# Moving the last six weight sums of layer 0 from the residual loads into the gates

## The chip, the cores and the metric

The kernel runs on one core of one Trainium2 chip. The metric is the device time of one execution in microseconds (us), as the median of several runs. A core has a matrix engine (PE, with PEld for its weight loads), a vector engine (DVE), a scalar engine (ACT), GpSimd (POOL) and a sync engine (SP). Each engine works its own queue of instructions in order. DMAs are issued from the queues of SP, ACT and POOL and are carried by 16 DMA engines that all of them share.

## What is computed

The reference is a trunk of two residual layers over 528 rows (16 meta tokens and 512 of the sequence) of width 2048. Layer 0 is a convolution branch and a sparse attention branch, each multiplied by a SiLU gate, put side by side and sent through one output projection. Layer 1 is a gated linear recurrence, which this change does not touch.

```python
def even_mixer(hn, w_in, conv_w, ...):
    glu_v, glu_g, gate_a, q, c, gate_b, qi, ki, wi = split_last(hn @ w_in, EVEN_SPLITS)
    ...
    a_out = jax.nn.silu(layer_norm(u, ln_g, ln_b)) * jax.nn.silu(gate_a)
    ...
    b_out = b_out * jax.nn.silu(gate_b)
    return jnp.concatenate([a_out, b_out], axis=-1) @ w_out

for layer in range(DEPTH):
    hn = rms_norm(h, norm_gain[layer])
    ...
    h = h + y
```

## The kernel before

All matrices are held transposed: 128 channels on the partitions, up to 528 rows along the free dimension. To keep fp32 precision, each operand is split into two fp16 halves (hi and lo), and a product is three matmuls (lines 270 to 272 in a "stripe", line 1069 in a "product" of 24 matmuls). A weight slab of 128 output channels comes from HBM into a `w32` buffer, is scaled and rounded by ACT (line 207, `wh`), and the rest is taken by DVE (line 209, `wl`).

**The output projection of layer 0** handles the 16 slabs of output channels as 8 pairs, with a scheme of seven products for each pair and half the rows where plain blocks would take eight (Strassen's, in Winograd's form). It needs sums and differences of weight blocks. These do not depend on the data, so DMAs with an added destination make them in HBM, in the tensors `esum` (the tile is called `es` in the profile): for each of the 8 pairs eight DMAs of 512 KB in six steps, 64 in all, in the list `later`. The last step of a pair adds a block of weights to its fourth sum. The list goes step by step over all pairs, so that its last six entries are the last step of pairs 2 to 7.

`send(todo, n, name)` (line 375) takes n entries from the front of a list and issues them on POOL. `behind(name)` orders them behind the instruction that was last noted as `queued[name]` on the same engine, and behind the sum before (`"W"`). It sets an order in the queue; it is no wait.

```python
def send(todo, n, name="G"):
    for _ in range(min(n, len(todo))):
        dst, src, add = todo.pop(0)
        with band(CONV), behind(name), behind("W"):
            queued["W"] = G.dma_start(dst, src, accum_op=OP.add if add else OP.bypass)
```

58 of the 64 go out during the scores, the convolution's stripes and the attention heads. The order of the engines' queues beyond such edges is chosen by a planner that simulates the program; `band(level)` gives priorities (weights 5, evacuations 4, side work 3, `CONV` 2).

**The gates** (lines 995 to 1014) are eight rounds, each with one stripe for `gate_a`, the finishing of one slab of the convolution branch, and the fp16 forms of both branches for the output projection (`attention_form`, `mixed_forms`). The attention output of a head was stored to HBM (`mbd`) and is reloaded by `stage(i)` (line 924, on POOL) into a freed buffer: heads 0 to 3 before the last head, head 4 in round 1, head 5 (tile `u`) in round 2, head 6 (tile `kih`) in round 6. What a reload overwrites has to be read first, which is what the DMA waits for.

**After the gates** the pools of layer 0 close (`ev.close()`), and new pools take their memory. `residual0` (line 1040) loads slabs of the residual x on POOL into tiles `h`; a load waits until the memory is free. Four are issued ahead of the projection, and behind the last of these stand the six sums that are left (line 1051). Then come the pairs. `pair_begin` loads a pair's first two half slabs (`half_load`, line 1060, on SP into halves of `w32`) and, from pair 2 on, two more into buffers of their own (`fourth`, line 1091). For pairs 0 and 1 the scale of the weights is known from earlier. From pair 2 on it is measured: ACT squares and sums the four blocks (line 191, tile `junk`), DVE adds the four sums (line 1112), POOL adds over the partitions (line 143). `pair_corner` does two of the seven products and `pair_rest` five; DVE adds each result to the residual (line 1076), and `first_square` squares it for the next norm (lines 1082 to 1086).

Of the kernel before, what the change touches and what calls it, by code (L numbers as in the profile page):

```python
# [74 lines left out]
def trunk_kernel(ctx: ExitStack, tc: tile.TileContext, x: bass.AP, w: bass.AP, wukv: bass.AP,  # L75
# [3 lines left out]
    V, S, G, P, Q = nc.vector, nc.scalar, nc.gpsimd, nc.tensor, nc.sync  # L79

    def band(level):
        return tc.high_priority(level * 1000000)
# [52 lines left out]
    def col(c):  # L135
        return vec[:, c:c + 1]
# [3 lines left out]
    queued = {}  # L140
# [71 lines left out]
    def behind(name):  # L212
        return tc.issue_after(queued[name].ins) if name in queued else ExitStack()
# [21 lines left out]
    def catch_up(last=False):  # L235

        tasks.sort(key=lambda v: v[:2])
        while tasks and (last or tasks[0][0] < clock[0]):
            us, _, job = tasks.pop(0)
            after = next((i for t, i in flow if t >= us), None)  # L240
            with tc.issue_after(after.ins) if after is not None else ExitStack():
                job()
            tasks.sort(key=lambda v: v[:2])
# [114 lines left out]
    mbd = dram.tile([HB, 128, T], F32, name="mbd")  # L358
# [4 lines left out]
    def sum_steps(sa, sb, d, first=0):  # L363

        k1, k2 = slice(first, first + 1024), slice(1024 - first, 2048 - first)
        a1, a2, b1, b2 = w[sa, :, k1], w[sa, :, k2], w[sb, :, k1], w[sb, :, k2]
        return [[(d[0], b1, 0), (d[2], a1, 0)], [(d[0], b2, 1), (d[2], b1, 1)], [(d[1], d[0], 0)],
                [(d[1], a1, 1)], [(d[3], d[1], 0)], [(d[3], a2, 1)]]
# [6 lines left out]
# [5 lines that stand above are left out]
# [7 lines left out]
    def et(shape, dt, name, bufs):  # L387
        return epools[EROLE.get(name, "es")].tile(shape, dt, name=name, bufs=bufs)
# [13 lines left out]
    with band(WGT + 1):  # L402
        for k in range(KT):
            shape, name, bufs = STAGE[k]
            hin = et(shape, F32, name, bufs)
            if len(shape) > 2:
                hin = hin.rearrange("p a b -> p (a b)")
            hin = hin[:, :T]
# [285 lines left out]
    def gate(s, name, keep=None, known=None):  # L694

        ps, inv = stripe(s, X0, back0, keep=keep, known=known)
        catch_up()
        dst = et([128, T], F32, name, 2)
        a = et([128, T], F32, "gt", 3)
        with band(EVAC):  # L700
            put(a, ps, inv)
            queued["T"] = S.activation(dst, a, AF.Tanh, scale=0.5)
            V.scalar_tensor_tensor(dst, dst, 1.0, a, op0=OP.add, op1=OP.mult)
        return dst
# [185 lines left out]
    def mix_scale():  # L890

        with band(SIDE):
            sums = cst([128, 8], F32, "mxb")
            for i in range(3):
# [15 lines left out]
    later = [t for step in zip(*[sum_steps(S_OE + 2 * p, S_OE + 2 * p + 1, d, 1024) for p, d in enumerate(esum)])  # L910
             for ts in step for t in ts]

    XA = [None] * 8

    def stage(i):

        if i == 7:
            XA[i] = MB[0]
            return
        shape, dt, name, bufs = (([128, CW - 1 + T], F32, "u", 2), ([128, T], F32R, "kih", 1),  # L920
                                 ([128, T], F32R, "kil", 1))[(0, 0, 1, 2, 0, 0, 1)[i]]
        XA[i] = et(shape, dt, name, bufs)[:, :T].bitcast(F32)
        with band(SIDE), behind("B5" if i < 4 else "B7"):
            G.dma_start(XA[i], mbd[i])

    for step in EVEN:
        what, i = step[0], int(step[1:])
        if step == "h7":
            for n in range(4):
                stage(n)  # L930
        if what == "n":
            layer_norm()
        else:
            {"g": glu, "s": scores, "k": select_later, "h": head}[what](i)
# [28 lines left out]
    def attention_form(i):  # L963

        x = XA[i]
        with band(SIDE):
            V.tensor_tensor(x[:, t2], x[:, t1], x[:, t2], op=OP.subtract)
            if i % 2 == 0:
                pairs_of.append(wide().bitcast(F16).rearrange("p (c a b) -> p c a b", c=2, a=2))
            PA[i] = split(pairs_of[-1][:, i % 2], x, mxq[1])  # L970

    def mixed_forms(i):

        x, z = XA[i], MA[i]
        with band(SIDE):
            PB[i] = split(form(), z, mxq[0])
            V.scalar_tensor_tensor(z[:, t2], x[:, t2], 2.0, z[:, t2], op0=OP.mult, op1=OP.add)
            V.scalar_tensor_tensor(x[:, t1], x[:, t1], 2.0, z[:, t2], op0=OP.mult, op1=OP.subtract)
            V.tensor_tensor(z[:, t1], z[:, t1], z[:, t2], op=OP.subtract)
            PC[i] = split(form(), z, mxq[0])  # L980
            if not parts:
                last = xp.tile([128, 2, T], F16, name="x", bufs=KT).rearrange("p a b -> p (a b)")
                parts.extend(last[:, c * T:(c + 1) * T].rearrange("p (a b) -> p a b", a=2) for c in range(2))
            PD[i] = split(form(True), x[:, t1], mxq[0])
# [11 lines left out]
    for i in range(8):  # L996
        ga = gate(S_GA + i, "qh", known=(gasc[:, i:i + 1], gainv[:, i:i + 1]))
        for n in ((), (4,), (5,), (), (), (), (6,), (7,))[i]:
            stage(n)
        if i < 6:  # L1000
            attention_form(i)
        with band(SIDE):
            z = Z[i]
            V.tensor_tensor(z, z, rz, op=OP.mult)
            S.activation(z, z, AF.Identity, scale=col(V_LG + i), bias=col(V_LB + i))
            th = et([128, T], F32, "gt", 3)
            S.activation(th, z, AF.Tanh, scale=0.5)
            V.scalar_tensor_tensor(z, th, 1.0, z, op0=OP.add, op1=OP.mult)
            V.tensor_tensor(z, z, ga, op=OP.mult)
        MA.append(z)  # L1010
        if i >= 6:
            attention_form(i)
        mixed_forms(i)
    catch_up(True)
    ev.close()


# [18 lines left out]
    HIN = []  # L1036

    def residual0(name="h1", bufs=12):
        hin = U.tile([128, T], F32, name=name, bufs=bufs)
        queued["R"] = G.dma_start(hin, x[len(HIN)])  # L1040
        HIN.append(hin)

    with band(EVAC), behind("B7"):
        residual0("h0", 2)
        residual0("h0", 2)
        acc1 = U.tile([128, T], F32, name="acc1", bufs=1)
        U.tile([128, 1024], F32, name="w4", bufs=4)
        U.tile([128, T], F32, name="sq1", bufs=2)
        residual0("h2", 2)
        residual0("h2", 2)  # L1050
    send(later, len(later), "R")

    spare = []

# [672 lines left out]
```

## Time and profile before

| | us |
|---|---|
| median of 3 runs | 1811.06 (1810.11 to 1812.9) |
| profiled execution | 1806.77 |
| its span | 1804.9 |
| PE busy | 1776.2 |
| DVE busy | 1422.1 |
| ACT busy | 1238.9 |
| POOL busy | 230.9 |

The profile is one execution. In its rows a line starts with the start of an instruction in us from the start of the span and its duration in us (or, in grouped rows, with busy sums), then the engine, the line of the kernel, the operation, and output <- inputs; "x2" is two such instructions in a row, and brackets at the end give the idle time of the engine before it and what ended that. "SPq" is SP's queue of DMA issues. DMA rows give the size and the time from issue to landing; q0 is POOL's queue of transfers, q1 is SP's. PEclk is the granted clock of PE as a share of full speed.

### The profile page before, as it was taken

The page shows a single profiled execution, that of the slowest core. Times are in us where ns is not written, and L with a number is a line of the kernel's source. Part 1 is how long each engine was busy: PE and PEld are TensorE (multiplying, and loading weights), DVE is VectorE, ACT ScalarE, POOL GpSimd, SP SyncE. Part 2 cuts the span into 40 slices and gives each one's busy share as a digit, 9 for nine tenths or more (in the row PEclk, how much of TensorE's full clock was granted, in tenths as well). Part 3 has the DMA queues.
Part 4 walks back from the last instruction along what each step waited for, and adds up shares of the span by engine and source line. Part 5 has one row for each costly group of instructions (what it writes and reads, how often), then busy time and mean ns, then how long its engine had stood idle before and what let it go on. Part 6 is the DMA issues. An engine that isn't in the chain of part 4 may idle for free.

```text
span 1804.9 us, 36999 instructions
## 1 busy us (share of the span) xinstructions
PE 1776.2 (98%) x14821; PEld 1371.3 (76%) x14821; DVE 1422.1 (79%) x2973; ACT 1238.9 (69%) x2049; POOL 230.9 (13%) x401
## 2 busy tenths in 40 slices
PE   9999999999999998999999999999999999999997
PEld 7675588888888886888777777777777765447885
DVE  7799999999897675777877777777777776767774
ACT  6755667666777654775777777877877767866562
POOL 1212301223221101100110001010100000002000
PEclk9999999999999999999999999999999999999998
DMA  6735784767864539774655555455654334567552
GB/s 239 215 124 181 195 223 124 214 192 232 218 213 147 150 112 283 253 252 149 214 169 161 171 167 175 141 163 166 176 162 140 120 106 176 204 215 268 200 197 96
DMA packets 80844, 329.54 MB, mean 183 GB/s; under 512 B 10432, under 2 KB 18024, under 8 KB 65472
## 3 DMA queue, kind: packets, MB, share of 16 engines
q1 hardware_dynamic: 40720, 189.93, 29.7%
q0 software_dynamic: 24832, 86.59, 20.1%
q10 hardware_dynamic: 15120, 50.66, 8.4%
q8 instruction: 116, 1.90, 0.4%
q14 instruction: 56, 0.46, 0.1%
HBM read 309.36 MB, written 73.87 MB: 212 GB/s over the span
## 4 chain that ended last, share of the span: by engine, by line
PE 92%; DVE 2%; DMA 2%; issue 1%; POOL 0%; ACT 0%; DVEq 0%; POOLq 0%
PE mps L271 21%; PE mps L272 21%; PE mps L270 21%; PE mps L1069 14%; PE s L726 1%; PE po L776 1%; DMA w<-es 1%; PE s L1251 1%; PE s L1250 1%; PE s L1252 1%; PE po L1377 1%; PE s L299 1%; PE mps L299 1%; PE po L1376 1%; PE s L601 1%
## 5 line engine op out<-in xcount | busy, mean ns | idle before, releaser
L272 PE MATMUL mps<-x,wl 128*128 128x264 f16 (+1 forms) x2912 | 869.3, 299 | 0.6 <-DVE wl L209 0.6
L271 PE MATMUL mps<-x,wh 128*128 128x264 f16 (+1 forms) x2912 | 869.2, 299 | 0.5 <-DVE x L329 0.4
L270 PE MATMUL mps<-x,wh 128*128 128x264 f16 (+1 forms) x2912 | 868.1, 299 | 0.0
L271 PEld LDWEIGHTS <-wh 128*128 128x128 f16 x2912 | 284.9, 98 | 105.9 <-issue 2.2
L272 PEld LDWEIGHTS <-wl 128*128 128x128 f16 x2912 | 285.0, 98 | 105.2 <-DVE wl L209 0.9
L270 PEld LDWEIGHTS <-wh 128*128 128x128 f16 x2912 | 285.2, 98 | 100.7 <-issue 0.5
L207 ACT ACTIVATE wh<-w,sc 128x1024 f16<-128x1024 f32 x216 | 245.4, 1143 | 124.8 <-PE mps L271 76.5
L209 DVE SCALAR_TENSOR_TENSOR wl<-w,sc,wh 128x1024 f16<-128x1024 f32 x216 | 275.2, 1278 | 41.0 <-ACT wh L207 40.0
L1069 PEld LDWEIGHTS <-wh 128*128 128x128 f16 x1808 | 177.2, 98 | 38.0 <-issue 12.2
L191 ACT ACTIVATE junk<-w 128x2048 bf16<-128x2048 f32 (+2 forms) x115 | 192.7, 1675 | 18.8 <-DMA w<-in_w_dram 18.0
L691 DVE SCALAR_TENSOR_TENSOR z<-u,vec,z 128x528 f32<-128x528 f32 x240 | 179.0, 758 | 1.1
L143 POOL PARTITION_ALL_REDUCE tot<-ss x79 | 44.3, 561 | 680.2 <-ACT junk L191 680.1
L1069 PEld LDWEIGHTS <-wl 128*128 128x128 f16 x904 | 88.9, 98 | 13.0 <-issue 0.2
L207 ACT ACTIVATE wh<-w,oq 128x1024 f16<-128x1024 f32 x53 | 60.7, 1147 | 51.2 <-PE mps L1069 43.2
L209 DVE SCALAR_TENSOR_TENSOR wl<-w,oq,wh 128x1024 f16<-128x1024 f32 x53 | 68.0, 1283 | 29.3 <-ACT wh L207 29.0
L1069 PE MATMUL mps<-on,wh 128*128 128x256 f16 (+2 forms) x464 | 78.1, 273 | 0.1
L1247 DVE SCALAR_TENSOR_TENSOR qlm<-q,qhm 128x256 f16<-128x256 f32 x128 | 52.5, 420 | 20.2 <-ACT qhm L1246 20.2
L191 ACT ACTIVATE junk<-gw 128x1024 bf16<-128x1024 f32 x64 | 66.9, 1045 | 1.4 <-DMA gw<-in_w_dram 1.1
L209 DVE SCALAR_TENSOR_TENSOR wl<-w,gsc,wh 128x1024 f16<-128x1024 f32 x32 | 41.0, 1282 | 33.1 <-ACT wh L207 33.0
L1246 ACT ACTIVATE qhm<-q 128x256 f16<-128x256 f32 x128 | 51.1, 411 | 22.2 <-DVE q L1352 18.6
L1069 PE MATMUL mps<-on,wl 128*128 128x256 f16 (+2 forms) x232 | 63.2, 273 | 0.0
L209 DVE SCALAR_TENSOR_TENSOR wl<-w,gaq,wh 128x1024 f16<-128x1024 f32 x30 | 38.4, 1280 | 22.9 <-ACT wh L207 22.8
(556 smaller groups left out, 3245.5 us busy)
## 6 DMA issues: line engine op xcount, KB each, us to landing
w<-in_w_dram SPq DMA_DIRECT2D x115, 1024.0 KB, 5.1
gw<-in_w_dram ACTq DMA_DIRECT2D x64, 512.0 KB, 6.5
es<-in_w_dram POOLq DMA_DIRECT2D x48, 512.0 KB, 10.9
w<-in_w_dram SPq DMA_DIRECT2D x45, 512.0 KB, 4.8
os<-in_w_dram POOLq DMA_DIRECT2D x42, 512.0 KB, 8.4
w<-es SPq DMA_DIRECT2D x32, 512.0 KB, 5.3
w<-os SPq DMA_DIRECT2D x28, 512.0 KB, 4.7
pa<-in_w_dram ACTq DMA_DIRECT2D x24, 512.0 KB, 4.4
```

The source lines that it names most:

```text
L143: queued["G"] = G.partition_all_reduce(out, src, channels=128, reduce_op=op or bass_isa.ReduceOp.add)
L191: S.activation(junk[:, :src.shape[-1]], src, AF.Square, accum_out=ss)
L207: queued["S"] = S.activation(hi, src, AF.Identity, scale=sc)
L209: V.scalar_tensor_tensor(lo, src, sc, hi, op0=OP.mult, op1=OP.subtract)
L270: P.matmul(o, hi[half][:, ws], xh[:, sl], start=n == 0 and k == 0, stop=False)
L271: P.matmul(o, hi[half][:, ws], xl[:, sl], start=False, stop=False)
L272: mm = P.matmul(o, lo[half][:, ws], xh[:, sl], start=False, stop=n == 1 and k == 7)
L299: queued["P"] = P.matmul(o[:m], rows[k], X[k][:, sl], start=k == 0, stop=k == KT - 1)
L691: V.scalar_tensor_tensor(z, u[:, j:j + T], col(V_CW + i * CW + j), z, op0=OP.mult, op1=OP.add)
L1069: P.matmul(p, wt[:, sl], xt, start=start and k == i == 0, stop=stop and k == 7 and i == 2, skip_group_check=stop and not start and resume)
L1246: S.activation(hi, src, AF.Copy, scale=scale)
L1247: V.scalar_tensor_tensor(lo, src, scale, hi, op0=OP.mult, op1=OP.subtract)
```

## The change

The six sums that are left go out in two groups of three during the gates: in round 2 behind the reload of head 5 (the sixth), and in round 6 behind the reload of head 6 (the seventh). For that, `stage` now notes its DMA as `queued["R"]`, and `residual0` no longer does. The call behind the residual loads is gone, and an assertion says that the list is empty. (Later code uses the name `"R"` again, after it has been set anew in `mean1`.)

```diff
         with band(SIDE), behind("B5" if i < 4 else "B7"):
-            G.dma_start(XA[i], mbd[i])
+            queued["R"] = G.dma_start(XA[i], mbd[i])
...
         for n in ((), (4,), (5,), (), (), (), (6,), (7,))[i]:
             stage(n)
+        if i in (2, 6):
+            send(later, 3, "R")
         if i < 6:
             attention_form(i)
...
     catch_up(True)
+    assert not later
     ev.close()
...
     def residual0(name="h1", bufs=12):
         hin = U.tile([128, T], F32, name=name, bufs=bufs)
-        queued["R"] = G.dma_start(hin, x[len(HIN)])
+        G.dma_start(hin, x[len(HIN)])
         HIN.append(hin)
...
         residual0("h2", 2)
         residual0("h2", 2)
-    send(later, len(later), "R")
```

## The prediction

> **What bounds the kernel now.** I read the page's busy shares first, then a table of stretches around the change, then the timelines of PE, DVE, ACT, SP and POOL at the one stretch where PE falls idle, and last the DMA view of that stretch.
>
> ```profile
> PE 1776.2 (98%) x14821; PEld 1371.3 (76%) x14821; DVE 1422.1 (79%) x2973; ACT 1238.9 (69%) x2049; POOL 230.9 (13%) x401
> ```
> ```profile
> core 0: us, PE busy (x) PEld busy (x) DVE busy (x) ACT busy (x) POOL busy (x), PEclk, DMA share, GB/s
> 660.00:713.00 53.00, 52.95 (x471) 45.90 (x470) 34.88 (x53) 25.13 (x32) 7.73 (x11) 1.00 0.70 201
> 713.00:729.00 16.00, 5.60 (x26) 3.78 (x26) 6.45 (x15) 9.76 (x15) 1.56 (x3) 0.57 0.80 294
> 729.00:830.00 101.00, 101.00 (x900) 87.80 (x899) 79.14 (x118) 72.36 (x96) 6.37 (x13) 1.00 0.70 239
> ```
>
> PE is the bound nearly everywhere (98%), so only what lets PE wait, or slows its clock, is worth anything. Between the last gate of layer 0 (ends at 677.6) and 830 there is one such place: 713 to 729, where PE is busy 5.6 us of 16 at a granted clock of 0.57. PE's timeline gives its price:
>
> ```profile
> 677.68 0.39 PE L1069 MATMUL mps<-pa,wh 128*128 128x264 f16 x2
> ...
> 683.09 0.39 PE L1069 MATMUL s<-pa,wh 128*128 128x264 f16 x2
> ...
> 712.67 0.28 PE L1069 MATMUL s<-Kh,wl 128*128 128x264 f16 x1
> 723.40 0.60 PE L1069 MATMUL s<-ch,wh 128*128 128x264 f16 x2 [10.45 <-DVE h L1076]
> ...
> 728.63 0.42 PE L1069 MATMUL mps<-pa,wh 128*128 128x264 f16 x1
> ```
>
> Two products of 24 matmuls run from 677.68 to 683.09, so one takes 2.70 us. The product after the gap takes 723.40 to 728.63 = 5.23 us, 2.53 more, at the lowered clock. The place costs 10.45 + 2.53 = 12.98 us. PE waited for an addition on DVE (line 1076, the reader of the bank). Why was that late?
>
> ```profile
> 720.55 0.71 DVE L1086 TENSOR_TENSOR acc<-acc,sq 128x528 f32<-128x528 f32 x1 [6.58 <-ACT sq L1085]
> 722.77 0.16 DVE L1112 TENSOR_REDUCE ss<-ss 128x1 f32<-128x4 f32 x1 [1.51 <-ACT junk L191]
> 722.85 0.49 DVE L1076 SCALAR_TENSOR_TENSOR h<-s,gaq,h 128x264 f32<-128x264 f32 x1
> ```
> ```profile
> 717.27 1.06 ACT L191 ACTIVATE junk<-w 128x1024 bf16<-128x1024 f32 x1 [5.42 <-DMA w<-in_w_dram]
> ```
>
> DVE works its queue in order: the addition stood behind an accumulation and a reduction, which waited for ACT, and ACT's queue stood at the first square sum (line 191) of the third pair of output weights, whose load had not landed. SP had issued the two half loads of that pair (weights and sum) long before:
>
> ```profile
> 693.77 0.33 SPq L1060 DMA_DIRECT2D w<-in_w_dram  x1
> 694.14 9.08 SPq L1060 DMA_DIRECT2D w<-es  x3
> ```
> The DMA view, narrowed to each of these two issues, gives 23.5 and 24.4 us to landing (717.3, 718.5); the same kinds between 725 and 760 take 4.9 and 5.9:
> ```profile
> w<-in_w_dram SPq DMA_DIRECT2D x1, 512.0 KB, 23.5
> ```
> ```profile
> w<-es SPq DMA_DIRECT2D x1, 512.0 KB, 24.4
> ```
> ```profile
> w<-es SPq DMA_DIRECT2D x8, 512.0 KB, 5.9
> w<-in_w_dram SPq DMA_DIRECT2D x6, 512.0 KB, 4.9
> ```
>
> What was in their way is the change's subject. POOL's timeline (two parts of it), and the DMA view of 690 to 723:
>
> ```profile
> 618.20 0.59 POOL L924 DMA_DIRECT2D u<-mbd  x1 [12.16 <-DVE uh L329]
> 634.04 0.55 POOL L924 DMA_DIRECT2D kih<-mbd  x1 [15.25 <-DVE uh L329]
> 634.58 0.54 POOL L1040 DMA_DIRECT2D h<-in_x_dram  x1
> 682.15 2.65 POOL L1040 DMA_DIRECT2D h<-in_x_dram  x5 [47.03 <-issue]
> 684.80 4.28 POOL L379 DMA_DIRECT2D es<-in_w_dram  x5
> 689.91 0.81 POOL L379 DMA_DIRECT2D es<-in_w_dram  x1 [0.83 <-DMA h<-in_x_dram]
> ```
> ```profile
> GB/s 418 413 303 258 268 273 288 273 263 288 253 209 273 263 273 278 283 273 278 273 263 283 278 268 263 293 258 273 263 303 367 387 432 412 422 427 417 395 405 310
> ...
> q0 software_dynamic: 974, 3.48, 50.5%
> q1 hardware_dynamic: 1731, 6.27, 49.4%
> ```
>
> The residual loads waited 47 us for their memory (the gates' pools), the six sums stood behind them, and went out at 684.8 to 690.7, just when SP was loading output weights. The DMA engines are then full for 33 us; POOL's queue (q0) takes 50.5% of them, SP's (q1) 49.4%. The 40 slices of the rate are 0.825 us each: about 270 GB/s up to the 30th (715 us), where the two queues share, and over 400 in the 33rd to 37th. The stall is thus six sums in SP's way.
>
> **The change, part by part.**
>
> *Taken away at 684.8.* The six sums leave that place. I estimate one from POOL's share: 50.5% of 33 us is 16.7 us of all engines, all of it sums apart from an end of the residual loads, so 2.8 us per sum. Without them the work from 682.15 to SP's issue at 694.14 is five residual loads (together 1.3 MB) and ten half loads (SP issues eight from 682.97 to 689.3, then these two): 5.2 MB. At 0.41 MB per us, the late slices, 6.6 MB need 16 us: all has landed by about 699, and the two cannot land before 693.77 + 4.9 = 698.7. So 699 to 700, not 717 to 718.5. To remove PE's wait wholly, 10.45 us earlier (706.8, 708.1) are enough; I get 18. Gain: the 10.45 us, and 2.53 of clock with it.
>
> *What is late next.* With the loads there at 700, ACT does the four square sums (1.06 us in the row above, with the read-out of the sum some 1.2) before 706, and the scales follow by about 708. PE, without a stop, ends the second pair at 677.68 + 14 x 2.70 = 715.5. Then it needs the third pair's first split, one ACT and one DVE pass (1.1 and 1.3 us): ready near 711. Cover: 4 us. The later pairs run in this manner from 729 to 830 with PE at 101.00 of 101. So I add nothing here.
>
> *POOL's issue time.* 4.28 + 0.81 us for six are moved, not added. Behind the first three POOL has nothing until 634.04, behind the other three one residual load and then a wait to 682.15: its cover is 12 us and over 40. Nothing. Their sources are weights, their targets were last written by copies issued by 602.8; no wait is added on POOL that anyone stands behind. The loads of the finished sums (SP) come after 702; with the sums done by about 655 they wait no more than now.
>
> *Added at 618.8: three sums behind the sixth head's reload (u).*
> ```profile
> 618.00:634.00 16.00, 15.09 (x147) 12.65 (x147) 11.63 (x27) 9.66 (x21) 0.59 (x1) 1.00 0.21 79
> 634.00:645.00 11.00, 11.00 (x100) 9.56 (x99) 8.69 (x14) 6.61 (x11) 1.08 (x2) 1.00 0.45 145
> 645.00:660.00 15.00, 15.00 (x135) 13.05 (x134) 11.88 (x18) 8.83 (x14) 0.00 (x0) 1.00 0.41 141
> ```
> The DMA engines are busy 0.21 of these 16 us, so 3 x 2.8 = 8.4 us fit. But the reload itself is on the path: the chain of waits goes from it over DVE to PE.
> ```profile
> 618.20 5.91 DMA u<-mbd
> ...
> 627.99 0.22 PE po L776
> ```
> ```profile
> u<-mbd POOLq DMA_DIRECT2D x1, 264.0 KB, 7.2
> ```
> Each microsecond that this reload is later is one on PE. Lower bound 0: it is issued ahead of the sums. Upper bound by the nearest row: the fifth head's reload (issued at 601.46, last fence) had mask reloads, a copy and two sums close behind it on the same queue, and took 7.2 us instead of 5.9: +1.3. The far end is a load wholly in the sums' company, 23.5 us: +17.6. I take the middle of the near ends, +0.65.
>
> The Trainium skill, "DMA: Bandwidth & Descriptors", section "Queues, rings and completion order", says that each DMA engine takes turns between queue rows and works one row's ring in its order. The trace agrees with the first (50.5% against 49.4%). By the second the reload would not be delayed at all, this term would be 0, and the sum 1798.1 instead of 1798.7.
>
> *Added at 634.6: three behind the seventh head's reload (kih).* It landed after 5.9 us at 639.9, and PE was busy 11.00 of 11 and 15.00 of 15 about it; what it feeds is used a gate (10.8 us) later. +1.3 is hidden. SP's half loads of 633 to 654 get slower, but are for splits from 656 on. If that cover went, the price would again be 1.3.
>
> *Sum:* -10.45 - 2.53 + 0.65 = -12.3 us. The profiled execution took 1806.8 (span 1804.9), 4.3 below the median of the runs: 1794.4 for such an execution, 1811.06 - 12.3 = 1798.7 for the median.
>
> **The rivals.**
>
> *Part of the stall stays (1805).* For it: even without the sums the ten loads and five residual loads come within 12 us, and keep the engines full up to about 699. If the two loads land at 711 (halfway), PE waits about 4 us and the clock loss of 2.5 stays: gain 13 - 6.5 - 0.65 = 6. Against: 18 us of lead for 10.45 needed. On the clock, the trace shows 0.57 after 10.45 us of idleness and 1.00 around the 0.4 us pause before 627.99. The Trainium skill, "TensorE: Matmul & The Clock Gate", Part 1, puts the limit at about 3.4 us of idleness; by it a remainder below that would cost no clock. No row here lies between.
>
> *The sums don't move as told (1799 to 1811).* The planner orders POOL's queue. If the second three come behind the second residual load, they still go out at 684.8: 8.4 us of engine time join the 16, the loads land by 707, the stall is 0 to 1 us, time 1799 to 1800. If all six stay: 1811. Against: the residual load waits 47 us for memory, the sums for nothing, and they are put behind the reloads by name.
>
> *The gain is taken back later (1811).* A later wait not paced by PE would have to swallow it. For it: DVE is 79% busy and in some stretches full. Against: PE is 101.00 of 101 behind the stall, its loads are released by splits that follow PE.
>
> *Slower: the sums hold up the sixth head's reload.* If it lands like the loads beside six sums, 23.5 us instead of 5.9, PE waits 17.6 us more at 628, and a clock loss of 2.5 joins: 20.1 - 13.0 = +7, 1818. It decides once that reload takes over about 16 us, when idleness and clock loss make up the 13.0. Against: 7.2 us in the nearest like case, and it is ahead in the queue.
>
> **How the numbers follow.** Forecast 0.63 (own range 1796 to 1802: the third term from 0 to 1.3, and 1.5 us either way, as the three runs scatter); part of the stall 0.17; not moved as told 0.06, half of it still near the forecast; taken back 0.07; slower 0.07. A measurement of this kernel tells 0.2% (3.6 us) from no change: faster means below 1807.4, slower above 1814.7. Faster: 0.63 + 0.17 + 0.03 = 0.83, less 0.01 for remainders above the halfway case: 0.82. Same: 0.07 + 0.03 + 0.01 = 0.11, slower 0.07. The range 1795.0 to 1806.5 holds the forecast and the partial case, and leaves out the rest.
>
> **What would show it.** Right: no idle row of PE between 677.7 and about 830; PEclk 1.00 there; the two loads that SP issues at 693.8 land in 5 to 8 us; six es rows of POOL in two threes behind the reloads of u and kih; the u reload at 5.9 to 7.2 us. Wrong: PE waits on DVE line 1076 again, a longer u reload with idle PE behind it at 628, or sums still beside 685.

## The result and the profile after

The changed kernel took 1795.83 us (median of 6 runs, 1794.1 to 1798.11), the kernel before 1811.98 beside it (6 runs, 1808.47 to 1813.75): a ratio of 0.9912, 95% interval 0.9899 to 0.9925, or 13.6 to 18.3 us less. A second comparison of the same two kernels (experiment 5) gave 0.9928 (0.9916 to 0.9940), 13.0 us. Ratios leave out a few executions that were slow as a whole, while each of the two medians of experiment 6 still counts one. The profiled execution took 1795.26 us, with a span of 1793.4.

The stretches of the changed kernel, with the columns as before (the first three in the gates, where the sums now are; then the projection):

```profile
core 0: us, PE busy (x) PEld busy (x) DVE busy (x) ACT busy (x) POOL busy (x), PEclk, DMA share, GB/s
618.00:634.00 16.00, 15.30 (x149) 12.74 (x148) 11.85 (x31) 9.92 (x23) 3.15 (x4) 1.00 0.81 185
634.00:645.00 11.00, 11.00 (x100) 9.56 (x99) 8.79 (x15) 5.91 (x10) 3.72 (x5) 1.00 0.86 204
645.00:660.00 15.00, 15.00 (x135) 13.05 (x134) 11.83 (x18) 10.03 (x16) 0.00 (x0) 1.00 0.64 203
...
660.00:713.00 53.00, 53.00 (x473) 46.10 (x472) 39.13 (x65) 31.75 (x44) 4.17 (x8) 1.00 0.60 216
713.00:729.00 16.00, 16.00 (x145) 13.91 (x143) 14.04 (x22) 13.79 (x19) 1.49 (x3) 1.00 0.75 264
729.00:830.00 101.00, 100.23 (x890) 86.95 (x888) 76.45 (x115) 63.70 (x85) 6.21 (x13) 1.00 0.63 216
```

From 713 to 729 PE is busy 16.00 of 16 us at a clock of 1.00, where it was 5.60 at 0.57. The 0.77 us that PE is idle between 729 and 830 are a pause at 822.3; the profile of before has it too, with 0.93 us at 834.3. In the gates the DMA engines are busier (0.81, 0.86 and 0.64 where 0.21, 0.45 and 0.41 stood) and PE is not less busy for it. The additional 9.6, 4.5 and 3.5 us of time of all engines make 17.5 for six sums, 2.9 for each; the estimate was 2.8.

POOL's timeline, and the DMA view of the same places (size, then time from issue to landing), show the sums in two threes behind the two reloads:

```profile
619.77 0.59 POOL L924 DMA_DIRECT2D u<-mbd  x1 [11.92 <-DVE uh L329]
620.35 2.57 POOL L379 DMA_DIRECT2D es<-in_w_dram  x3
635.40 0.58 POOL L924 DMA_DIRECT2D kih<-mbd  x1 [12.48 <-DVE uh L329]
635.97 2.57 POOL L379 DMA_DIRECT2D es<-in_w_dram  x3
637.56 1.56 POOL L1043 DMA_DIRECT2D h<-in_x_dram  x1
683.52 0.57 POOL L1043 DMA_DIRECT2D h<-in_x_dram  x1 [44.40 <-issue]
684.27 2.12 POOL L1043 DMA_DIRECT2D h<-in_x_dram  x4 [0.18 <-issue]
```
```profile
es<-in_w_dram POOLq DMA_DIRECT2D x3, 512.0 KB, 9.5
...
u<-mbd POOLq DMA_DIRECT2D x1, 264.0 KB, 5.7
...
es<-in_w_dram POOLq DMA_DIRECT2D x3, 512.0 KB, 11.1
...
kih<-mbd POOLq DMA_DIRECT2D x1, 264.0 KB, 5.8
h<-in_x_dram POOLq DMA_DIRECT2D x1, 264.0 KB, 13.8
```

The reload of the sixth head lands after 5.7 us (5.9 before), that of the seventh after 5.8 (5.9 before): neither pays. The residual load issued behind the second three takes 13.8 us, and nobody needs it for 40.

The two half loads of the third pair are issued by SP at 695.12 and 695.49:

```profile
695.12 0.33 SPq L1062 DMA_DIRECT2D w<-in_w_dram  x1
695.49 9.08 SPq L1062 DMA_DIRECT2D w<-es  x3
```
```profile
w<-in_w_dram SPq DMA_DIRECT2D x1, 512.0 KB, 8.3
w<-es SPq DMA_DIRECT2D x1, 512.0 KB, 9.2
```

They land at 703.4 and 704.7, that is 8.3 and 9.2 us after their issue and not 23.5 and 24.4. What follows, on ACT, DVE and PE:

```profile
704.93 1.04 ACT L191 ACTIVATE junk<-w 128x1024 bf16<-128x1024 f32 x1
...
709.24 1.06 ACT L191 ACTIVATE junk<-w 128x1024 bf16<-128x1024 f32 x1
```
```profile
710.42 0.16 DVE L1114 TENSOR_REDUCE ss<-ss 128x1 f32<-128x4 f32 x1 [0.99 <-ACT junk L191]
...
711.74 0.48 DVE L1078 SCALAR_TENSOR_TENSOR h<-s,gaq,h 128x264 f32<-128x264 f32 x1
```
```profile
679.04 0.39 PE L1071 MATMUL mps<-pa,wh 128*128 128x264 f16 x2
...
714.14 0.39 PE L1071 MATMUL s<-ch,wh 128*128 128x264 f16 x2
...
716.84 0.39 PE L1071 MATMUL mps<-pa,wh 128*128 128x264 f16 x2
```

The first square sum carries no wait in brackets now. The addition that frees PE's bank (line 1078, before 1076) still stands behind the reduction, but ends at 712.2, 1.9 us before PE needs it at 714.14. From the first product of the output projection (679.04) to the first of the third pair (716.84) PE takes 37.80 us, exactly 14 products of 2.70. Before, it was 677.68 to 728.63 = 50.95. This **stretch** from product to product is 13.15 us shorter; I use it below, since it is read inside one execution. The two spans differ by 11.5 only because the profile of before reached the projection 1.36 us earlier and took 0.29 less behind the stretch (1076.27 against 1076.56).

### The profile page after: what moved, and what is told of

Read it like the earlier page. It is cut to its first block, busy times and chain, and to the rows that moved or that the text cites. A ratio compares the mean times of both kernels' runs of the same rounds, so it can differ in the third digit from the quotient of the medians.

```text
span 1793.4 us, 37001 instructions
## 1 busy us (share of the span) xinstructions
PE 1774.7 (99%) x14821; PEld 1370.6 (76%) x14821; DVE 1423.5 (79%) x2973; ACT 1238.8 (69%) x2049; POOL 231.6 (13%) x401
## 4 chain that ended last, share of the span: by engine, by line
PE 87%; DVE 4%; DMA 2%; ACT 2%; issue 2%; POOL 1%; DVEq 0%; SPq 0%; ACTq 0%; POOLq 0%
PE mps L271 20%; PE mps L270 20%; PE mps L272 20%; PE mps L1071 14%; PE s L726 1%; PE po L776 1%; PE s L1071 1%; DVE wl L209 1%; PE s L1252 1%; PE s L1253 1%; PE s L1254 1%; PE po L1379 1%; PE po L1378 1%; PE s L601 1%; ACT junk L191 1%
## 5 line engine op out<-in xcount | busy, mean ns | idle before, releaser
L191 ACT ACTIVATE junk<-w 128x2048 bf16<-128x2048 f32 (+2 forms) x115 | 192.6, 1675 | 13.8 <-DMA w<-in_w_dram 13.0
L1339 DVE COPY_PREDICATED A<-msk,s 128x256 f32<-128x256 uint8 x96 | 46.6, 485 | 10.6 <-PE s L1254 10.3
```

The lines of the kernel that those rows point to most:

```text
L191: S.activation(junk[:, :src.shape[-1]], src, AF.Square, accum_out=ss)
L1339: V.copy_predicated(A.rearrange("p b (n a m) -> p b n a m", a=2, m=mm)[:, :, :, 1, :], msk[:, li - 1 + i:li + i, :].rearrange("p b (n m) - ...
```

## The experiments

Each ratio is to the kernel before, run beside it on the same chip, with its 95% interval. "Loads" are the two half loads of the third pair, counted from their issue. Stretch is as just defined.

| kernel | ratio (interval) | median us | loads land after, us | stretch us |
|---|---|---|---|---|
| 1 before, again | 0.9997 (0.9988 to 1.0006) | 1809.36 | 23.4, 24.3 | 50.92 |
| 2 no sums | 0.9912 (0.9898 to 0.9927) | 1793.96 | 7.9, 8.8 | 37.80 |
| 3 six small | 0.9918 (0.9905 to 0.9932) | 1795.3 | 10.0, 10.9 | 37.80 |
| 4 three moved | 0.9933 (0.9919 to 0.9946) | 1797.96 | 15.5, 16.4 | 42.07 |
| 5 changed, again | 0.9928 (0.9916 to 0.9940) | 1795.41 | 7.9, 8.7 | 37.80 |
| 6 reload behind | 0.9943 (0.9929 to 0.9956) | 1798.73 | not read | not read |
| 6 again | 0.9935 (0.9919 to 0.9950) | 1797.79 | 8.4, 9.2 | 37.79 |
| 7 three to six more | 1.0022 (1.0013 to 1.0031) | 1812.41 | 24.4, 26.7 | 53.00 |

### 1. The kernel before, again

No edit: is the stall a constant of that kernel?

> The kernel before once more, unchanged: ratio 1.000 within 0.002. Its profile is what is wanted. The changed kernel gained 16 us by the medians but 11.5 us between the two profiled executions, and the stall of PE in the profile of before was worth 13.0. Theory A (the stall is what was gained, and it differs from run to run with how the transfers fall): this second profile shows the same stall of PE on the same addition, worth something between 12 and 18 us. Theory B (the stall is always 13.0 and the other 3 us come from somewhere else): again 13.0 within 0.5, and the profiled execution nearer 1811 for another reason, somewhere before or behind the stall.

PE's row at the same place:

```profile
725.26 0.60 PE L1069 MATMUL s<-ch,wh 128*128 128x264 f16 x2 [10.42 <-DVE h L1076]
```

10.42 us, where the first profile had 10.45, and a stretch of 50.92 against 50.95, though this execution took 2.8 us longer (1809.60). The stall is the same in both; they differ elsewhere.

### 2. Without the six sums

```diff
-    send(later, len(later), "R")
+    later.clear()
```

The six sums are left out (their share of the projection's weights is missing).

> The kernel before without its last six sums (the last step of the fourth weight sum of pairs 2 to 7 is left out, all else stays). Theory A (the six transfers of 512 KB are what delays the weight loads): as fast as the changed kernel, ratio 0.991 within 0.0015, no idle row of PE near 713, the third pair's two loads land in 8 to 10 us. If the sums cost the reload of the sixth head 0.65 us in the changed kernel, this one is 0.65 us faster still. Rival (the gain comes from another order of the queues that the planner chose in the changed kernel): little or no gain, ratio above 0.997.

PE's first product of the projection, and its first of the third pair:

```profile
679.85 0.39 PE L1069 MATMUL mps<-pa,wh 128*128 128x264 f16 x2
...
717.65 0.39 PE L1069 MATMUL mps<-pa,wh 128*128 128x264 f16 x2
```

The stretch is 37.80 and the ratio 0.9912, as in the changed kernel. So the sums cause the whole stall, and in their new place they cost nothing that these comparisons can tell (0.9912 and 0.9928 with the sums among the gates, 0.9912 without any).

### 3. Six small sums in the old place

```diff
+    later = [(dst[:, :128], src[:, :128], add) for dst, src, add in later]
     send(later, len(later), "R")
```

Each adds only 128 of its 1024 columns. The six issues on POOL, their order and their waits stay.

> The kernel before with its last six sums at their old place, each cut to 128 of 1024 columns (the other seven eighths of these sums are left out): six issues on POOL, one eighth of the bytes. Theory A (bytes in flight beside SP's loads): nearly the whole gain, ratio 0.991 to 0.993. Rival (six more instructions at that place in POOL's queue, or their waits, are what hurts): no gain, ratio above 0.997.

POOL's timeline, and the DMA view of the six:

```profile
685.99 4.28 POOL L379 DMA_DIRECT2D es<-in_w_dram  x5
691.33 0.81 POOL L379 DMA_DIRECT2D es<-in_w_dram  x1 [1.06 <-DMA h<-in_x_dram]
```
```profile
es<-in_w_dram POOLq DMA_DIRECT2D x6, 64.0 KB, 12.7
```

POOL spends the same 4.28 + 0.81 us on them, at the same place, and the stall is gone (the stretch is 37.80, from 678.89 to 716.69). It was the traffic, not POOL's time or order.

### 4. Three moved, three at the old place

```diff
-        if i in (2, 6):
+        if i == 2:
             send(later, 3, "R")
...
-    assert not later
...
-        G.dma_start(hin, x[len(HIN)])
+        queued["H"] = G.dma_start(hin, x[len(HIN)])
...
+    send(later, len(later), "H")
```

The name `"H"` puts the last three behind the residual loads.

> The changed kernel with only the first three sums among the gates; the other three are issued behind the residual loads, as all six were before. By the prediction's working 3 sums leave 8.4 us less of transfers in the way, the two loads land by about 707 and PE waits 0 to 1 us: ratio 0.991 to 0.9925. Rival (the loss is in proportion to the bytes): half of the gain, ratio 0.9955 within 0.001, with an idle stretch of PE of 5 us or so.

PE at the place, the window, and the landing of the two loads (issued at 695.06 and 695.43):

```profile
716.69 0.54 PE L1071 MATMUL s<-ch,wh 128*128 128x264 f16 x2 [2.45 <-DVE h L1078]
...
719.66 0.43 PE L1071 MATMUL s<-L,wl 128*128 128x264 f16 x1
...
720.27 0.28 PE L1071 MATMUL s<-L,wl 128*128 128x264 f16 x1
...
721.05 0.39 PE L1071 MATMUL mps<-pa,wh 128*128 128x264 f16 x2
```
```profile
713.00:729.00 16.00, 13.55 (x107) 11.05 (x105) 12.42 (x20) 14.73 (x22) 1.54 (x3) 0.89 0.79 261
```
```profile
w<-in_w_dram SPq DMA_DIRECT2D x1, 512.0 KB, 15.5
```
```profile
w<-es SPq DMA_DIRECT2D x1, 512.0 KB, 16.4
```

Three sums in SP's way cost 2.45 us of idleness, and the product behind takes 716.69 to 721.05 = 4.36 us, 1.66 more than 2.70; together the stretch is 4.27 longer. The slow matmuls (0.43 us for one, 0.28 at full clock) last to about 719.9. The expectation, a ratio of 0.991 to 0.9925 with 0 to 1 us of waiting, was missed, and so was its rival, half of the gain.

Counted from the first product of the projection, the first load lands 24.38 us later in the changed kernel (703.42 - 679.04). In experiment 4 it is 31.58, in experiment 1 39.48 and in the profile of before 39.59. So it is late by 7.20, 15.10 and 15.21 us, and PE is idle 2.45, 10.42 and 10.45: each time 4.7 to 4.8 us less. That is the cover of this place (how late the loads may be before PE waits), and past it PE waits one for one. In experiment 3 the load is 1.7 us late (694.97 + 10.0 - 678.89 = 26.08), and PE does not wait.

### 5. The changed kernel, again

> The changed kernel once more. All profiles so far agree on the stretch from PE's first product of the output projection to the third pair's first product: 50.95 and 50.92 us with the six sums there, 37.80 without. Theory A (the whole gain is this 13.1 us): ratio 0.9927 within 0.0010. Theory B (outside the profile the stall is some 3 us longer, or something else is gained too): ratio 0.9912 again.

13.0 us by the medians (1808.36 to 1795.41), with an interval of 10.9 to 15.2. This agrees with the stretch's 13.15. The first comparison's 16 does not quite: its interval (13.6 to 18.3) begins just above the stretch. Experiment 4 gained 9.8 to 14.7 us by its interval, where its stretch is 8.9 shorter. The profiles show no further gain: outside the stretch the three with the stall of six sums (before, experiments 1 and 7) took 1754.0, 1756.7 and 1756.1 us, the changed kernel and experiments 2 to 5 between 1755.0 and 1756.0. Where the rest of those medians comes from stays open.

### 6. The reload behind the sums

The first three sums go ahead of the sixth head's reload, not behind it (a memset of one column stands in front, so that they start no earlier than the reload did):

```diff
+        if i == 5:
+            with band(SIDE), behind("B7"):
+                queued["R"] = G.memset(XA[i][:, :1], 0.0)
+            send(later, 3, "R")
-        with band(SIDE), behind("B5" if i < 4 else "B7"):
+        with band(SIDE), behind("W" if i == 5 else "B5" if i < 4 else "B7"):
...
-        if i in (2, 6):
+        if i == 6:
```

> The changed kernel with the first three sums issued just ahead of the sixth head's reload instead of just behind it (a one-column memset of the reload's buffer, ahead of them, makes them wait for the same moment). Theory A (transfers of POOL's queue are served in the order of issue, so that the reload was free of the sums only because it was ahead): the reload lands about 9 us later (14 to 16 us instead of 5.7), PE waits at the last head's values for 7 to 9 us more and loses 1 to 2.5 us of clock with it: 8 to 11 us slower than the changed kernel, ratio to before about 0.997 to 0.999. Rival (transfers of one queue share the engines whatever their order): no difference, ratio as the changed kernel's.

The profile of this run cannot be compared with the others, so I ran it once more:

> The run before this one once more (first three sums issued just ahead of the sixth head's reload): its profile came from an execution at a granted clock of 0.556 for all of its span and can't be compared. Its times gave 0.9943, 2.7 us slower than the changed kernel, where 8 to 11 were expected. Theory A (served in order, but part of the delay is covered): the reload lands 6 to 9 us later than 5.7, PE waits at the last head's values some 3 us more than in the changed kernel, and the stretch from the first product to the third pair stays 37.80. Theory C (the reload is hardly later): it lands within 2 us of 5.7, and the loss shows elsewhere.

POOL's timeline, the DMA view, DVE's reader of the reload, and PE's list of waits between 540 and 860:

```profile
618.90 2.49 POOL L379 DMA_DIRECT2D es<-in_w_dram  x3
620.48 1.51 POOL L928 DMA_DIRECT2D u<-mbd  x1
```
```profile
u<-mbd POOLq DMA_DIRECT2D x1, 264.0 KB, 12.6
```
```profile
633.21 0.43 DVE L971 TENSOR_TENSOR u<-u 128x264 f32<-128x264 f32 x1 [6.63 <-DMA u<-mbd]
```
```profile
PE mps L270 <- ACT gt L309: 2.8, 2, 2.2
```
```profile
600.00:660.00 60.00, 56.80 (x512) 48.33 (x511) 42.30 (x84) 36.50 (x69) 13.01 (x18) 1.00 0.74 179
```

Behind three sums the reload takes 12.6 us, ahead of them 5.7. The place in the queue decides. The Trainium skill, "DMA: Bandwidth & Descriptors", section "Queues, rings and completion order", says of the queues of SP and ACT that a DMA engine takes what stands in a ring in the ring's order. This trace agrees, on POOL's queue: behind, 6.9 us more; ahead, none. The time was my miss: the expectation charged the delay to PE, and the ratios lie only 0.0007 and 0.0015 above experiment 5's, 1.3 and 2.7 us, the intervals overlapping. In the profile PE is busy 56.80 of the 60 us in the gates, 59.29 in the changed kernel, and waits 2.8 us for ACT in two stripes instead. The planner had put other work (the splits of `pt`, line 752) ahead of the reload's reader on DVE, so a good part of the 7 us was covered.

### 7. Six transfers more at the old place

```diff
+    more = [dram.tile([128, 1024], F32, name=f"more{i}") for i in range(3)]
...
+    later += [(more[i], w[S_OE + 2 * i, :, 1024:], n) for n in range(2) for i in range(3)]
     send(later, len(later), "R")
```

Six transfers of 512 KB that nobody reads are queued behind the six sums: three copies, then three sums onto them.

> The kernel before with six more transfers behind its six sums at the old place: three copies and three sums of 512 KB into scratch that nobody reads. With three sums at this place the two loads of the third pair land in 15.5 and 16.4 us, with six in 23.5 and 24.4, with none in 8.3 and 9.2: 2.4 us for each sum. Theory A (the loads wait for a share of the engines as long as POOL's queue is full): they land 10 to 14 us later still, PE stands still 8 to 14 us longer, ratio 1.005 to 1.008. Rival (the loads were bound by something else that the sums only touch, so the loss is at its full size already): ratio within 0.002 of 1.

PE at the place, POOL's timeline, and the DMA queues between 690 and 723:

```profile
726.05 0.60 PE L1072 MATMUL s<-ch,wh 128*128 128x264 f16 x2 [12.50 <-DVE h L1079]
```
```profile
692.87 0.54 POOL L381 DMA_DIRECT2D more<-in_w_dram  x1 [1.26 <-DMA h<-in_x_dram]
694.80 0.53 POOL L381 DMA_DIRECT2D more<-in_w_dram  x1 [1.39 <-DMA h<-in_x_dram]
698.16 0.52 POOL L381 DMA_DIRECT2D more<-in_w_dram  x1 [2.83 <-DMA es<-in_w_dram]
...
728.15 2.58 POOL L381 DMA_DIRECT2D more<-in_w_dram  x3 [0.81 <-issue]
```
```profile
q0 software_dynamic: 1401, 5.06, 62.5%
q1 hardware_dynamic: 1412, 5.13, 40.9%
```

The stall grows by 2.05 us only, where the expectation had 8 to 14; the ratio lies just past its rival's bound of 0.002. POOL got three of the six out before 728, the last at 698.16, each behind an earlier landing; the other three stand in its queue behind the reduction for the scale (line 143), which ran at 725.76. But the first three land 27.6, 28.1 and 28.0 us after their issue, from 720.5 on, so POOL's queue was never empty before the two loads landed (718.8 and 721.4), and by the order seen in experiment 6 the other three would have come behind. In the kernel before, the last sum lands at 716.8 (26.9 us after 689.91), 0.5 us ahead of the first load and 1.8 ahead of the second. So six sums share the engines with SP nearly as long as the loads take, and more of them find little left to delay: SP's queue keeps 40.9% of the engines, where it had 49.4%. That is a reading of these times and shares; no run tests it by itself.

By the first load the wait is longer than the cover would have it (16.1 us late, 12.50 idle); by the second, 17.5 late, it is 5.0 less, near the 4.7 that this load too gives in experiments 1 and 4.

## Why the prediction was right

**The stall and its cause** stood as read: 10.45 + 2.53 us. Measured, 13.15 of the stretch went. The remaining 0.17 is the last matmul ahead of the stop: with no other behind it, it counts with its full 0.28 us and not with 0.11. Experiments 2 and 3 show the cause: the six sums' bytes, not POOL's issues.

**The landing.** I had 699 to 700; it was 703.4 and 704.7, of which 1.4 us is this execution's later start. The rest is in the step "at 0.41 MB per us, the late slices": in the changed kernel's DMA view of 683 to 705 the rate is 0 to 123 GB/s in the first 2.2 us and 217 to 338 from there to 689.6, with the residual loads among the others; only behind that is it about 400 (383 to 447). The 18 us of lead were really 15.2, with 10.45 needed; the step was off in size and the margin held it. The sign that I gave, 5 to 8 us from issue, was missed too, with 8.3 and 9.2.

**What is late next.** The cover of 4 us lies near the 4.7 to 4.8 of experiments 1 and 4, but that is luck. It was counted from loads at 700; they landed later, and 4.7 to 4.8 is what was left even then. By another sentence of the prediction, loads at 706.8 are enough, and that is right: 703.4 + 4.75 is 708.2 here, 706.8 with the earlier start of before. The order told there was not quite what happened. The addition at line 1076 stays behind the reduction in the changed kernel too, and it is this that has the least left, 1.9 us; the first split is ready at 714.1 and has 2.8.

**The sixth head's reload.** This term, +0.65, is the mis-sized one: it landed after 5.7 us, so it was 0. I had taken the middle between the queue's order (0) and the fifth head's 7.2. The rule that gave 1798.1 was right, and experiment 6 shows the other side of it.

**The sum.** -12.33 us by its terms; the stretch gave -13.15, of which 0.65 is the reload and 0.17 that last matmul, and experiment 5's medians -13.0. The result's 1795.83 us lies 2.9 below 1798.7; these two make 0.8 of that. The other 2.1 no run explains: in experiments 1 and 5 the kernel before took 1809.36 and 1808.36, less than the start of the sum (1811.06), but beside the result it took 1811.98.

**The rivals.** That part of the stall stays needed a landing over 4.75 us later than it was; it was not so. "The sums don't move as told" was priced wrong: with three at the old place I had the loads by 707 and a stall of 0 to 1 us; experiment 4 has them at 710.6 and 711.8 (1.3 of it from a later start), and the price is 4.27. The 8.4 us that the step added for three sums were not too little (7.2 measured); it added them to the landing that was already too early, and it gave the rest of the wait no clock loss, where 1.66 us came on top of 2.45. Taken back later: the rest of the program behind the stretch took 1076.15 to 1077.1 us in every profile of experiments 1 to 4 and of the two kernels. Slower by the reload: the mechanism exists (12.6 us behind the sums), but its price of one for one was too high.

**The clock.** Of a short remainder I said that no row lies between 0.4 and 10.45 us of idleness. The profile of before has some (0.79 us ahead of 626.65 and 0.93 ahead of 835.22, both at a clock of 1.00), and experiment 4 has the one that matters: after 2.45 us the granted clock over the window is 0.89 and the product takes 4.36 us. The Trainium skill, "TensorE: Matmul & The Clock Gate", Part 1, has a limit of about 3.4 us; this trace does not agree, and the measurement decides. Nor can 2.45 us be taken for a limit. In experiment 7 PE stands still from 713.55 on, and slices of 1 us (columns as before) show the full clock up to 718:

```profile
717.00:718.00 1.00, 0.00 (x0) 0.00 (x0) 0.00 (x0) 0.00 (x0) 0.00 (x0) 1.00 1.02 381
718.00:719.00 1.00, 0.00 (x0) 0.00 (x0) 0.00 (x0) 0.24 (x1) 0.00 (x0) 0.56 1.03 397
```

By such slices the clock falls 2.4 us after PE stops in the profile of before, 2.1 in experiment 1, 2.5 in experiment 4 and 4.6 in experiment 7. In experiment 4 that is 0.1 us behind PE's new start. What sets the moment no run shows.

## What to carry to other kernels

A DMA that nobody waits for still takes its share of the engines; it belongs where the DMA share is low, not where another queue is loading what comes next, and its place among the gates cost nothing at shares of 0.64 to 0.86. Put it behind an urgent transfer on the same queue: ahead of it, three of 512 KB made a reload 6.9 us later, behind it they cost nothing. To size such a stall, find the cover first (here 4.75 us), then charge PE one for one past it, and add the clock.

## What was not expected of the hardware

- 2.45 us of idleness was enough to lower PE's clock in experiment 4: 1.66 us lost in the next product, against 2.53 after 10.45 us. A pause of 2.15 us (the longest in the repeat of experiment 6, ahead of 650.53) and one of 1.92 (experiment 1, ahead of 837.92) left it at 1.00. The clock fell 2.1 to 4.6 us after PE's stop, so the cost of a pause of this length may differ from one execution to the next; no run repeats it.
- The delay is not linear in the number of sums. Over the 8.3 us of a free queue, three sums make the load 7.2 us later and six 15.2, but three more of the same size only 0.9 (first load) and 2.3 (second).
- POOL's issue of a DMA can wait for the landing of an earlier one (1.26, 1.39 and 2.83 us in experiment 7). In the trace POOL's DMAs report their landing on eight semaphores in turn, and each of the three waited for the DMA eight places before it, whose semaphore it uses again. The wait is thus the program's own; no run shows a limit of the queue.
